# Seven-product matrix steps: another order of the products, and room for weight tiles counted by the tiles in use

## The chip, the cores and the metric

The kernel runs on one core of a Trainium2 chip. The metric is device time in microseconds of one execution, as the median of several runs. Matrix products run on PE (its weight loads are shown as PEld); VectorE (DVE), ScalarE (ACT) and GpSimd (POOL) do the element-wise work; SyncE (SP) issues the transfers (DMA) between device memory and the core's memory SBUF. Matrix products write to PSUM, from which DVE and ACT read.

## What is computed

One layer of a hybrid decoder, for a prompt of 2048 tokens and 8 requests with 4 new tokens each (32 "sample" tokens), with 1024 features, in float32:

```python
h = x + mixer(rmsnorm(x))                # gated linear attention and a spatial gate, w_in, w_out
h = h + mem_attend(rmsnorm(h))           # attention over 256 memory tokens
g = hn @ w_gate                          # hn = rmsnorm(h); w_gate, w_up: 1024 x 2816
c = conv_b + sum(conv_w[j] * gp[:, j:j + T] for j in range(3))   # gp: two older rows, then g
h = h + (gelu(c) * (hn @ w_up)) @ w_down
y = rmsnorm(h)
```

The change lies in the products with `w_gate` and `w_up`.

## The kernel before

**Tiling.** The prompt is worked through in four blocks of 512 tokens (block 0 to 3). Activations stand with features on the 128 partitions and tokens along a row. Every float32 operand is split into a high part, rounded to the format that PE takes at full rate, and a low rest; `mm3` (lines 92 to 95) adds three products: high × high (L93), high × low (L94), low × high (L95). A split takes ACT for the high part (L85) and DVE for the rest (L86). The sample tokens go through the feed-forward part with block 2, whose rows are then 544 tokens long; their memory attention (`sqp`, `kTp`, `ssc`, a softmax `sp`, `sop`) is spread through the feed-forward part of block 1 as side work.

**Seven products.** In blocks 1 to 3 the products with `w_gate` (`gate7`, names `wg<block><step>`) and `w_up` (`upp7`, names `wup<block><step>`) take a form with seven block products in place of eight. A step yields two tiles of 128 output features for all tokens of the block; there are 11 steps of each kind per block. The weights of a step are three plain tiles (A11, A12, A22, stored by block 0 already split, names ending in `A`) and four sums (S1 with S4, S2 with S3: two raw tiles, names `w_…S`, which are split after loading). The tokens stand in two halves of H columns (256, or 272 in block 2) and in sums of them (`w1`, `wb`, `wu`, `wt`). `seven_step` (line 222) makes one `Step` per product, `part` (line 282):

- the products add up in four chains, x: A11, S2, S3; y: S1, S4; z: A12; w: A22. Each product is 12 matmuls (4 slices × 3).
- With H = 256 (`joint`: blocks 1 and 3) x and w share one bank of PSUM, z and y another, so a step holds two of the four banks `acc`; with 272 columns each chain has its own. A bank carries the name of the chain that is opened first in it. The first matmul in a bank clears it (`fresh`, L297).
- After A11, S1, S2 and A22, ACT copies the chain as it then stands into a quarter of the result (L304); after S3 and S4, DVE adds x to both tiles' halves (L310) and y and z to the first tile (L313). Then `use` runs: gate, convolution and GELU, or the product of the two branches.
- The first gate step of each block (`early`) has an order and code of its own, and the first up step runs `then` after S1: it makes the scale of the tokens' norm and lets the first gate's result go on.

**What sets the order.** The code lists steps (`run`, line 516); the framework then orders the instructions of each engine by its own estimate and may put another step's product between two of one step. A matmul that writes a bank and a copy that reads that bank are kept apart, also where they touch different columns. All transfers of weights are issued by SP, in a fixed order (`fetch`, line 107), each when the tile that it fills is free.

**Room for weights.** There are NW = 10 SBUF tiles for weights ready to use and NR = 4 for raw ones. `run` walks over the steps and, ahead of them, makes units of weights. A plain tile takes 1 of the 10, a split one 2 (`ring`). It notes for each unit the count of tiles made up to it, and stops when the tiles made since the oldest unit still in use would pass 10: a unit that is done counts as long as an older one is in use. A sums unit is in use until its second product (`until`). Raw units that are used without a split (`held`) are counted in the same way against the 4.

Of the kernel before, what the change touches and what calls it, by code (L numbers as in the profile page):

```python
# [13 lines left out]
ALU = mybir.AluOpType  # L14
# [16 lines left out]
NU, NT, NW, NR = 49, 8, 10, 4  # L31
# [6 lines left out]
def hymba_step_kernel(  # L38
# [10 lines left out]
    act, dve, pool, pe = nc.scalar, nc.vector, nc.gpsimd, nc.tensor  # L49
# [21 lines left out]
    def acc(name):  # L71
        return accp.tile([128, 512], F32, tag="acc", name=name)
# [24 lines left out]
    def W(name):  # L97
        return wp.tile([128, 1024], F32R, tag="w", name=name)

    def unit_of(make, ring=2, raw=None, held=False):  # L100

        return NS_(make=make, ring=ring, raw=raw, held=held, until=None)

    in_turn = mybir.DependencyInfo(mybir.DependencyClass.NoSync, mybir.DependencyReason.DATA)
    before = []
# [54 lines left out]
    def seven_tile(src, name):  # L160

        def load():
            t = W(name).rearrange("p (x k m) -> p x k m", x=2, k=4)
            fetch(t.bitcast(F32), src)
            return t
        return unit_of(load, 1)
# [47 lines left out]
    def sums_unit(src, k, name):  # L214

        def raw():
            t = raw_tile(name)
            fetch(t, src)
            return t.rearrange("p (k m) -> p k m", k=k)
        return unit_of(lambda raw: wsplit(raw, name), 2, raw)  # L220

    def seven_step(plain, sums, get_xs, H, outs, use, name, early=False, then=None):


        seq = ("A11", "S1", "A12", "S2", "S3", "S4", "A22") if early else ("A11", "A12", "S2", "S1", "A22", "S3", "S4")
        joint = 2 * H <= 512
        tiles = {}

        def unit(nm):
            if nm in PLAIN:  # L230
                return seven_tile(plain[:, PLAIN.index(nm)], f"{name}{nm}")
            i = SUMS.index(nm)
            return sums_unit(sums[:, i:i + 2].rearrange("p s k m -> p (s k m)"), 8, f"{name}{nm}")

        def hold(nm, w):
            if nm in PLAIN:
                tiles[nm] = w[:, 0], w[:, 1]
            else:
                for j in range(2):
                    tiles[SUMS[SUMS.index(nm) + j]] = tuple(w[x][:, 4 * j:4 * j + 4] for x in range(2))  # L240

        def mm(bank, nm, k, fresh, stop):
            wh, wl = tiles[nm]
            mm3(bank, wh[:, k], wl[:, k], *get_xs()[k][nm], fresh, stop, not early)

        def quarters(q):
            return [q[i // 2][:, (i % 2) * H:(i % 2 + 1) * H] for i in range(4)]

        loads = [nm for nm in seq if nm in PLAIN or SUMS.index(nm) % 2 == 0]
        last = 3  # L250

        if early:
            def fn(*ws):
                for nm, w in zip(loads, ws):
                    hold(nm, w)
                q = outs()
                q0, q1, q2, q3 = quarters(q)
                ps = {nm: (mps if i > 3 else acc)(f"a_{name}{nm}")[:, :H] for i, nm in enumerate(seq)}
                for nm in seq:
                    for k in range(last):  # L260
                        mm(ps[nm], nm, k, k == 0, False)
                for nm in seq:
                    mm(ps[nm], nm, last, False, True)
                    if nm == "A11":
                        act.activation(q0, ps[nm], AF.Copy)
                    elif nm == "S2":
                        dve.tensor_tensor(q3, ps[nm], q0, ALU.add)
                        dve.tensor_tensor(q0, ps["A12"], q0, ALU.add)
                    elif nm == "S3":
                        dve.tensor_tensor(q1, ps["S1"], q3, ALU.add)  # L270
                        dve.tensor_tensor(q2, ps[nm], q3, ALU.add)
                        dve.tensor_tensor(q3, ps[nm], q1, ALU.add)
                    elif nm == "S4":
                        dve.tensor_tensor(q1, ps[nm], q1, ALU.add)
                    elif nm == "A22":
                        dve.tensor_tensor(q2, ps[nm], q2, ALU.add)
                use(*q)
            return Step(fn, [unit(nm) for nm in loads])

        st = NS_()  # L280

        def part(nm, *ws):
            i = CHAIN[nm]
            if nm in loads:
                hold(nm, *ws)
            if nm == "A11":
                st.q, st.at = outs(), {}
            if i not in st.at:
                if joint:
                    t = acc(f"a_{name}{i}")  # L290
                    for n, o in enumerate("xw" if i in "xw" else "zy"):
                        st.at[o] = t[:, n * H:(n + 1) * H]
                    if i in "zy":
                        st.zy = t[:, 0:2 * H]
                else:
                    st.at[i] = acc(f"a_{name}{i}")[:, :H]
            fresh = nm in ("A11", "A12") or not joint and nm in ("S1", "A22")  # L297
            for k in range(last + 1):
                mm(st.at[i], nm, k, fresh and k == 0, k == last)
            if then and nm == "S1":  # L300
                then()
            q = st.q
            if nm in COPIED:
                act.activation(quarters(q)[COPIED[nm]], st.at[i], AF.Copy)  # L304
            elif nm == "A12" and not joint:
                q0 = quarters(q)[0]
                dve.tensor_tensor(q0, st.at["z"], q0, ALU.add)
            elif nm == "S3":
                q23 = q[1].rearrange("p (s t) -> p s t", s=2)
                dve.tensor_tensor(q23, st.at["x"].unsqueeze(1).broadcast_to([128, 2, H]), q23, ALU.add)  # L310
            elif nm == "S4":
                if joint:
                    dve.tensor_tensor(q[0], st.zy, q[0], ALU.add)  # L313
                else:
                    q1 = quarters(q)[1]
                    dve.tensor_tensor(q1, st.at["y"], q1, ALU.add)
                use(*q)

        parts = {nm: Step(lambda *ws, nm=nm: part(nm, *ws), [unit(nm)] if nm in loads else []) for nm in seq}
        for nm in SUMS[::2]:  # L320
            parts[nm].units[0].until = parts[SUMS[SUMS.index(nm) + 1]]
        return Step(None, parts=list(parts.values()))
# [65 lines left out]
    for l in range(7):  # L388
# [3 lines left out]
        v = mf[:, :64].rearrange("p (n h) -> p n h", h=half)  # L392
# [100 lines left out]
    class Step:  # L493
        def __init__(self, fn, units=(), parts=None):
            self.fn, self.units = fn, [wunit(*u) if isinstance(u, tuple) else u for u in units]
            self.parts = parts or [self]
# [19 lines left out]
    def run(steps):  # L516


        steps = [p for st in steps for p in st.parts]
        index = {st: i for i, st in enumerate(steps)}  # L520
        queue = [(i, u) for i, st in enumerate(steps) for u in st.units]
        raws = [(i, u) for i, u in queue if u.raw]
        ready, ring, held, loaded = {}, [], [], {}
        made = at = nraw = done = 0

        def fetched(upto):

            nonlocal nraw
            while nraw < min(upto, len(raws)):
                i, u = raws[nraw]  # L530
                if held and nraw - held[0][0] >= NR:
                    break
                if u.held:
                    held.append((nraw, index[u.until] if u.until else i))
                loaded[id(u)] = u.raw()
                nraw += 1

        for i, st in enumerate(steps):
            now[0] = i
            flush(i - 1)  # L540
            for live in (ring, held):
                while live and live[0][1] < i:
                    live.pop(0)
            while at < len(queue):
                j, u = queue[at]
                if ring and made + u.ring - ring[0][0] > NW:
                    break
                if u.raw:
                    fetched(done + 2)
                    if id(u) not in loaded:  # L550
                        break
                    done += 1
                if u.ring:
                    ring.append((made, index[u.until] if u.until and not u.held else j))
                ready.setdefault(j, []).append(u.make(*([loaded.pop(id(u))] if u.raw else [])))
                made += u.ring
                at += 1
            assert len(ready.get(i, ())) == len(st.units)
            st.fn(*ready.pop(i, []))
# [1327 lines left out]
```

## Time and profile before

| what | us |
|---|---|
| median of 3 runs | 2861.88 (2861.6 to 2862.01) |
| the profiled execution | 2856.59 |
| its span, first to last instruction | 2854.9 |
| PE busy in the span | 2803.4 (98%) |
| DVE, ACT, POOL busy | 1844.4, 1215.6, 576.0 |

How to read the rows. In a list of groups or of waits, `PE a_wg36x L93 <- DMA wg36A<-w7g` says that line 93 on PE, writing `a_wg36x`, stood idle until the transfer into `wg36A` had landed; then come the total, the number and the longest in microseconds. `a_wg36x` is the bank opened by chain x of gate step 6 of block 3. In a time line a row has the start in microseconds, the duration, engine, line, operation, output and inputs, shapes and count, and in brackets the idle time before it and what ended it. In a table by stretches a row has the stretch, its length, then busy time and number of instructions of PE, PEld, DVE, ACT and POOL, the granted clock of PE as a share of the full one, the busy share of the DMA engines and their GB/s.

### The profile page before, as it was taken

What the parts mean: (1) busy time and instruction counts of PE and PEld (TensorE: products, weight loads), DVE (VectorE), ACT (ScalarE), POOL (GpSimd) and SP (SyncE); (2) the same over time, 40 slices, a digit from 0 to 9 for tenths busy, and PEclk for the clock granted to TensorE, in tenths of its full rate; (3) what the DMA queues carried; (4) which work ended last, traced back from release to release, by engine and by line L of the source; (5) the groups of instructions that cost most, each with busy time, mean ns of one, the idle gap of its engine ahead of it and who ended that gap; (6) DMA issues with size and microseconds to landing.
All of it is one profiled execution on the core that took longest, in us unless ns stands there. A gap on an engine that the chain in (4) does not pass through costs nothing.

```text
span 2854.9 us, 46641 instructions
## 1 busy us (share of the span) xinstructions
PE 2803.4 (98%) x17894; PEld 2476.6 (87%) x17894; DVE 1844.4 (65%) x3054; ACT 1215.6 (43%) x2185; POOL 576.0 (20%) x638
## 2 busy tenths in 40 slices
PE   8999999999999999999999999999999999999998
PEld 8888888888878898888888879899999888899997
DVE  6588767677646876555455777755556776655565
ACT  5645543323453354333334445533333544533333
POOL 2002112111111321222220121322221122132232
PEclk9999999999999999999999999999999999999999
DMA  9766589999732255776885216566665324566664
GB/s 302 231 191 222 180 272 310 322 313 315 257 98 68 86 187 187 285 251 227 284 303 176 82 45 221 184 227 233 216 236 192 92 69 139 194 236 216 241 242 164
DMA packets 348212, 592.03 MB, mean 207 GB/s; under 512 B 25610, under 2 KB 225388, under 8 KB 347990
## 3 DMA queue, kind: packets, MB, share of 16 engines
q1 hardware_dynamic: 347990, 589.06, 61.3%
q8 instruction: 141, 2.31, 0.3%
q14 instruction: 81, 0.66, 0.1%
HBM read 473.09 MB, written 115.87 MB: 206 GB/s over the span
## 4 chain that ended last, share of the span: by engine, by line
PE 84%; DMA 5%; DVE 5%; ACT 2%; issue 1%; POOL 1%; SPq 0%; POOLq 0%; ACTq 0%; DVEq 0%
PE d L95 6%; PE d L94 6%; PE d L93 6%; PE a_wx L93 2%; PE a_wx L95 2%; PE a_wx L94 2%; PE s L1101 2%; PE a_wg L93 1%; PE a_wg L95 1%; PE a_wup L93 1%; PE a_wup L95 1%; PE a_wg L94 1%; PE a_wup L94 1%; PE a_wo L93 1%; PE a_wu L93 1%
## 5 line engine op out<-in xcount | busy, mean ns | idle before, releaser
L93 PE MATMUL d<-acth,h_wd 128*128 128x512 f32 (+1 forms) x864 | 303.8, 353 | 0.9 <-DMA h_wd<-wd 0.9
L94 PE MATMUL d<-actl,h_wd 128*128 128x512 f32 (+1 forms) x864 | 302.4, 350 | 0.0
L95 PE MATMUL d<-acth,l_wd 128*128 128x512 f32 (+1 forms) x864 | 302.3, 351 | 0.0
L1736 DVE TENSOR_TENSOR h<-d,h 128x512 f32<-128x512 f32 (+1 forms) x232 | 134.8, 584 | 154.9 <-PE d L95 154.2
L93 PEld LDWEIGHTS d<-acth,h_wd 128*128 128x128 f32 x864 | 162.3, 188 | 22.5 <-PE sqp L1446 1.4
L95 PEld LDWEIGHTS d<-acth,l_wd 128*128 128x128 f32 x864 | 162.2, 188 | 22.4 <-issue 0.8
L94 PEld LDWEIGHTS d<-actl,h_wd 128*128 128x128 f32 x864 | 162.5, 188 | 21.3 <-issue 0.8
L1631 POOL TENSOR_TENSOR c<-c,bc_f 128x512 f32<-128x512 f32 (+1 forms) x88 | 128.8, 1469 | 130.3 <-ACT c L1630 130.2
L1621 ACT ACTIVATE c<-g,colsb 128x512 f32<-128x512 f32 x88 | 70.4, 811 | 125.9 <-DVE g L1582 83.3
L1653 POOL TENSOR_TENSOR c<-q,c 128x512 f32<-128x512 f32 (+1 forms) x33 | 46.5, 1411 | 377.6 <-DVE q L310 261.0
L93 PE MATMUL a_wo<-ch,h_wo 128*128 128x512 f32 (+1 forms) x320 | 114.0, 367 | 0.7 <-ACT ch L89 0.4
L94 PE MATMUL a_wo<-cl,h_wo 128*128 128x512 f32 (+1 forms) x320 | 113.4, 357 | 0.0
L95 PE MATMUL a_wo<-ch,l_wo 128*128 128x512 f32 (+1 forms) x320 | 112.4, 355 | 0.0
L85 ACT ACTIVATE acth<-c 128x512 fp32r<-128x512 f32 (+1 forms) x88 | 55.4, 636 | 129.6 <-POOL c L1653 50.8
L1618 POOL COPY carry<-g 128x2 f32<-128x2 f32 x88 | 42.9, 492 | 324.4 <-DVE g L1582 276.0
L95 PE MATMUL a_wx<-pTh,l_wx 128*128 128x512 f32 x256 | 100.2, 394 | 0.0
L94 PE MATMUL a_wx<-pTl,h_wx 128*128 128x512 f32 x256 | 99.9, 393 | 0.0
L93 PE MATMUL a_wx<-pTh,h_wx 128*128 128x512 f32 x256 | 99.0, 394 | 0.0
L86 DVE TENSOR_TENSOR actl<-c,acth 128x512 fp32r<-128x512 f32 (+1 forms) x88 | 63.9, 728 | 39.8 <-ACT acth L85 39.2
L1622 DVE SCALAR_TENSOR_TENSOR c<-g,colsb,c 128x512 f32<-128x512 f32 x88 | 72.1, 827 | 14.7 <-ACT c L1621 14.6
L1630 ACT ACTIVATE c<-c 128x512 f32<-128x512 f32 (+1 forms) x88 | 55.0, 634 | 56.9 <-DVE c L1623 53.8
L1623 DVE SCALAR_TENSOR_TENSOR c<-g,colsb,c 128x512 f32<-128x512 f32 x88 | 76.7, 881 | 1.2
(4117 smaller groups left out, 9542.8 us busy)
## 6 DMA issues: line engine op xcount, KB each, us to landing
h_wd<-wd SPq DMA_DIRECT2D x66, 512.0 KB
l_wd<-wd SPq DMA_DIRECT2D x66, 512.0 KB
w_wo<-in_w_out_dram SPq DMA_DIRECT2D x32, 512.0 KB
h_wx<-vod SPq DMA_DIRECT2D x32, 512.0 KB
l_wx<-vod SPq DMA_DIRECT2D x32, 512.0 KB
w_wg<-in_w_gate_dram SPq DMA_DIRECT2D x22, 512.0 KB
w_wup<-in_w_up_dram SPq DMA_DIRECT2D x22, 512.0 KB
w_wd<-in_w_down_dram SPq DMA_DIRECT2D x22, 512.0 KB
```

The lines of the kernel that those rows point to most:

```text
L85: act.activation(hi, src, AF.Copy)
L86: (lo_eng or dve).tensor_tensor(lo, src, hi.bitcast(F32), ALU.subtract)
L93: pe.matmul(ps, wh, xh, start=first, stop=False, skip_group_check=again)
L94: pe.matmul(ps, wh, xl, start=False, stop=False, skip_group_check=again)
L95: pe.matmul(ps, wl, xh, start=False, stop=last, skip_group_check=again)
L1101: pe.matmul(ps3[:, :, c * 64:(c + 1) * 64], kl[:, c * 128:(c + 1) * 128], kr3[:, :, c * 64:(c + 1) * 64], start=True, stop=True)
L1621: act.activation(c[:, :SB], g[:, 2:SB + 2], AF.Identity, bias=cb, scale=w2)
L1622: dve.scalar_tensor_tensor(c[:, :SB], g[:, 1:SB + 1], w1, c[:, :SB], ALU.mult, ALU.add)
L1623: dve.scalar_tensor_tensor(c[:, :SB], g[:, 0:SB], w0, c[:, :SB], ALU.mult, ALU.add)
L1630: act.activation(c[:, :T], c[:, :T], AF.Gelu_apprx_tanh)
L1631: pool.tensor_tensor(c[:, :T], c[:, :T], B.fbc[:, :T], ALU.mult)
L1736: dve.tensor_tensor(B.h[m + mm][:, cs], ps[:, :cw], B.h[m + mm][:, cs], ALU.add)
```

## The change

Two things change.

**The order of the products** in `seven_step`, outside the early step: from A11, A12, S2, S1, A22, S3, S4 to A11, S1, A12, A22, S2, S4, S3. The first four each begin a chain, the last three add to one. With it go which product clears a bank, and the end of a step: the addition of y (and z) follows S4 and is no longer last, the addition of x to both tiles follows S3, and `use` runs there. The bank that was named z is now opened by y. Weights are loaded in the order of their use, so S1's raw tile is now loaded before S2's.

**The count of room**: `ring` and `held` become tables of the units in use with the step up to which each is; a new unit fits when the tiles of the units in use and its own are at most 10 together. A raw unit that is held counts from when it is taken up, together with the raw tiles loaded and not yet taken. For this a unit becomes an object of a class of its own. Line numbers shift by 3 or 4.

```diff
-        seq = (... "S4", "A22") if early else ("A11", "A12", "S2", "S1", "A22", "S3", "S4")
+        seq = (... "S4", "A22") if early else ("A11", "S1", "A12", "A22", "S2", "S4", "S3")
...
-            fresh = nm in ("A11", "A12") or not joint and nm in ("S1", "A22")
+            fresh = nm in ("A11", "S1") or not joint and nm in ("A12", "A22")
...
+            elif nm == "S4" and joint:
+                dve.tensor_tensor(q[0], st.zy, q[0], ALU.add)
+            elif nm == "S4":
+                q1 = quarters(q)[1]
+                dve.tensor_tensor(q1, st.at["y"], q1, ALU.add)
             elif nm == "S3":
                 q23 = q[1].rearrange("p (s t) -> p s t", s=2)
                 dve.tensor_tensor(q23, st.at["x"].unsqueeze(1).broadcast_to([128, 2, H]), q23, ALU.add)
-            elif nm == "S4":
-                if joint:
-                    dve.tensor_tensor(q[0], st.zy, q[0], ALU.add)
-                else:
-                    q1 = quarters(q)[1]
-                    dve.tensor_tensor(q1, st.at["y"], q1, ALU.add)
                 use(*q)
...
-                if held and nraw - held[0][0] >= NR:
+                if len(held) + nraw - done >= NR:
                     break
...
             for live in (ring, held):
-                while live and live[0][1] < i:
-                    live.pop(0)
+                for u in [u for u in live if live[u] < i]:
+                    del live[u]
...
-                if ring and made + u.ring - ring[0][0] > NW:
+                until = index[u.until] if u.until else j
+                if ring and sum(v.ring for v in ring) + u.ring > NW:
                     break
...
-                if u.ring:
-                    ring.append((made, index[u.until] if u.until and not u.held else j))
+                ring[u] = j if u.held else until
```

The instructions of every engine are the same in kind and number. Up to block 1's feed-forward part their order is the same too, but for a few transfers that trade neighbours; from there on it differs within the feed-forward parts of blocks 1, 2 and 3.

More of the change, by code (lines that the diff above doesn't have):

```diff
@@ L98, in W, with __init__ @@
         return wp.tile([128, 1024], F32R, tag="w", name=name)
+    class Unit:
+        def __init__(self, make, ring, raw, held):
+            self.make, self.ring, self.raw, self.held, self.until = make, ring, raw, held, None
     def unit_of(make, ring=2, raw=None, held=False):
-        return NS_(make=make, ring=ring, raw=raw, held=held, until=None)
+        return Unit(make, ring, raw, held)
     in_turn = mybir.DependencyInfo(mybir.DependencyClass.NoSync, mybir.DependencyReason.DATA)
@@ L222, in seven_step @@
     def seven_step(plain, sums, get_xs, H, outs, use, name, early=False, then=None):
-        seq = ("A11", "S1", "A12", "S2", "S3", "S4", "A22") if early else ("A11", "A12", "S2", "S1", "A22", "S3", "S4")
+        seq = ("A11", "S1", "A12", "S2", "S3", "S4", "A22") if early else ("A11", "S1", "A12", "A22", "S2", "S4", "S3")
         joint = 2 * H <= 512
@@ L522, in run @@
         raws = [(i, u) for i, u in queue if u.raw]
-        ready, ring, held, loaded = {}, [], [], {}
-        made = at = nraw = done = 0
+        ready, loaded = {}, {}
+        ring, held = {}, {}
+        at = nraw = done = 0
         def fetched(upto):
@@ L530, in fetched @@
                 i, u = raws[nraw]
-                if held and nraw - held[0][0] >= NR:
+                if len(held) + nraw - done >= NR:
                     break
-                if u.held:
-                    held.append((nraw, index[u.until] if u.until else i))
-                loaded[id(u)] = u.raw()
+                loaded[u] = u.raw()
                 nraw += 1
@@ L549, in run @@
                     fetched(done + 2)
-                    if id(u) not in loaded:
+                    if u not in loaded:
                         break
                     done += 1
-                if u.ring:
-                    ring.append((made, index[u.until] if u.until and not u.held else j))
-                ready.setdefault(j, []).append(u.make(*([loaded.pop(id(u))] if u.raw else [])))
-                made += u.ring
+                    if u.held:
+                        held[u] = until
+                ring[u] = j if u.held else until
+                ready.setdefault(j, []).append(u.make(*([loaded.pop(u)] if u.raw else [])))
                 at += 1
```

## The prediction

> **What bounds the kernel now.** I read the page first, then the idle time of each engine in the stretches that the change touches, then the chain of waits of PE, then single rows on the time line.
>
> ```profile
> span 2854.9 us, 46641 instructions
> PE 2803.4 (98%) x17894; PEld 2476.6 (87%) x17894; DVE 1844.4 (65%) x3054; ACT 1215.6 (43%) x2185; POOL 576.0 (20%) x638
> PE 84%; DMA 5%; DVE 5%; ACT 2%; issue 1%; POOL 1%; SPq 0%; POOLq 0%; ACTq 0%; DVEq 0%
> ```
>
> PE is busy 2803.4 of 2854.9 us and holds 84% of the chain that ended last. The change adds and removes no matmul, copy, addition or byte, so it can only move PE's idle time. The seven-product form is used in the feed-forward parts of blocks 1, 2 and 3 (`a_wg1…`, `a_wup1…` and so on). Their three stretches, with PE's busy time first:
>
> ```profile
> 1120.00:1500.00 380.00, 368.13 (x2811) 325.84 (x2810) 204.31 (x253) 136.13 (x233) 92.51 (x108) 1.00 0.76 267
> 1825.00:2115.00 290.00, 289.64 (x2314) 289.23 (x2314) 170.91 (x289) 111.11 (x199) 82.25 (x119) 1.00 0.62 222
> 2490.00:2805.00 315.00, 310.20 (x2227) 290.57 (x2227) 181.65 (x224) 118.29 (x197) 89.10 (x89) 1.00 0.67 233
> ```
>
> PE idles 380 - 368.1 = 11.9 us in block 1, 0.4 us in block 2 and 4.8 us in block 3: 17 us in all, which is nearly the ceiling of what the change can give. What ended these waits (total, times, longest):
>
> ```profile
> PE a_wup15x L93 <- ACT q L304: 3.1, 1, 3.1
> PE a_wg36x L93 <- DMA wg36A<-w7g: 1.5, 1, 1.5
> PE a_wg16z L93 <- DVE g L310: 1.2, 1, 1.2
> PE a_wg16z L95 <- DVE l_wg16S L86: 1.2, 1, 1.2
> ...
> PE a_wup32z L93 <- ACT q L304: 0.9, 1, 0.9
> PE a_wup110x L93 <- ACT q L304: 0.8, 1, 0.8
> PE a_wg18z L93 <- DMA wg18A<-w7g: 0.8, 1, 0.8
> PE a_wup19x L93 <- ACT q L304: 0.7, 1, 0.7
> PE a_wg18x L93 <- DMA wg18A<-w7g: 0.7, 1, 0.7
> PE a_wg34x L93 <- DMA wg34A<-w7g: 0.7, 1, 0.7
> PE a_wg14z L93 <- DMA wg14A<-w7g: 0.6, 1, 0.6
> ...
> PE a_wg310x L93 <- DMA wg310A<-w7g: 0.5, 1, 0.5
> PE a_wup13x L93 <- DMA wup13A<-w7u: 0.5, 1, 0.5
> PE a_wg32x L93 <- DMA wg32A<-w7g: 0.5, 1, 0.5
> PE a_wg38x L93 <- DMA wg38A<-w7g: 0.5, 1, 0.5
> PE a_wg12x L93 <- DMA wg12A<-w7g: 0.4, 1, 0.4
> ```
>
> Two kinds matter: weights that land late (DMA), and a copy or addition out of PSUM that comes late (ACT, DVE). The idle column understates each wait:
>
> ```profile
> 2652.68 0.28 PE L94 MATMUL a_wup35z<-wtlwx,h_wup35S 128*128 128x256 f32 x1
> 2652.80 0.28 PE L95 MATMUL a_wup35z<-wthwx,l_wup35S 128*128 128x256 f32 x1
> 2654.62 0.36 PE L93 MATMUL a_wg36x<-w1wx,wg36A 128*128 128x256 f32 x1 [1.55 <-DMA wg36A<-w7g]
> ```
>
> Matmuls start 0.12 us apart but are shown 0.28 us long. The stall is 2654.62 - 2652.80 - 0.12 = 1.70 us where 1.55 is listed, so I add 0.16 to each wait. One product is 12 matmuls, 1.4 us.
>
> **Loads ahead of the gate products, block 3.** The transfers of gate pair 36 left SP's queue thus:
>
> ```profile
> 2648.71 0.80 SPq L109 DMA_DIRECT2D wg36A<-w7g  x2
> 2649.55 0.42 SPq L109 DMA_DIRECT2D w_wg36S<-s7g  x1
> 2650.07 0.38 SPq L109 DMA_DIRECT2D w_wup36S<-s7u  x1
> 2657.93 0.32 SPq L109 DMA_DIRECT2D wg36A<-w7g  x1
> ```
>
> Four transfers of 512 KB (A11, A12, S1, the next S2) start within 1.4 us, and A11 is there only when PE goes on at 2654.6: 5.9 us for a load that shares the DMA engines with three others. SP's queue at this place, before and after (A11, A12, A22 are the plain tiles, S1 and S2 the sums, g the gate, u or up the up-projection):
>
> ```order
> L109 DMA w_wup35S1_27078<-s7u5_198 128x1024
> L109 DMA w_wg36S2_27149<-s7g6_200 128x1024
> L109 DMA wup35A22_27155<-w7u5_197 128x1024
> L109 DMA wg36A11_27186<-w7g6_199 128x1024
> L109 DMA wg36A12_27188<-w7g6_199 128x1024
> L109 DMA w_wg36S1_27206<-s7g6_200 128x1024
> L109 DMA w_wup36S2_27277<-s7u6_202 128x1024
> L109 DMA wg36A22_27283<-w7g6_199 128x1024
> ```
>
> ```order
> L113 DMA wup35A22_27110<-w7u5_197 128x1024
> L113 DMA w_wg36S1_27151<-s7g6_200 128x1024
> L113 DMA wg36A11_27157<-w7g6_199 128x1024
> L113 DMA w_wg36S2_27188<-s7g6_200 128x1024
> L113 DMA wg36A12_27210<-w7g6_199 128x1024
> L113 DMA wg36A22_27238<-w7g6_199 128x1024
> L113 DMA w_wup36S1_27279<-s7u6_202 128x1024
> ```
>
> S1 now goes ahead of A11, and A12 no longer rides beside it. The programs' semaphores tell which matmul frees the tile that a load takes over. For A11 of gates 34, 36, 38 little changes: 37 matmuls lie between that one and A11's own first before, 38 after (36 for gate 310, 49 for 32 both times). So the count by tiles in use does not bring A11 forward; what changes is its company. A12 is freed 28 matmuls (3.3 us) after A11, so A11 and S2 share the engines alone. By bytes, half of four transfers' 5.9 us is 3 us; the bounds are 3.0 and 5.9, and I take 4.0, since part of the 5.9 is not transfer but start and finish. The lead is 38 × 0.12 = 4.6 us. The five waits (1.5, 0.7, 0.5, 0.5, 0.5, plus 5 × 0.16 = 4.5 us) shrink to some 0.5: gain **4.0** (bounds 0 and 4.5).
>
> **Loads, block 1.** By the same counts gates 12 (third plain tile), 14 (A12) and 18 (A12) get 57 or more matmuls of lead and lose 0.4 + 0.6 + 0.8 + 0.5 = **2.3** (bounds 1 and 2.3). `wg18` A11 and `wup13` A11 keep theirs (36 and 42 matmuls). Two leads get short: A11 of gate 16 has 28 matmuls, 3.3 us (48 before), and the last down-projection's low tile in block 3 has 26. Against 4.0 us needed I charge **0.5** each; the far bound is 5.9 - 3.2 = 2.7 each.
>
> **Copies out of PSUM.** For 256 tokens a step has two banks: x|w and z|y. A product that adds to a bank must wait for the copy that reads it. In the new list A12 follows S1 and S2 follows A22 in one bank; before, S3 followed A22. The order fills these places: counted on PE's queue in blocks 1 and 3, waits on a copy or addition less than 2.6 us after the product that it reads go from 27 + 3 to 10 + 5. `wup19` loses its wait (three products and narrow work now lie between A11 and A22, two before between A11 and S2): 0.7 + 0.16 = 0.9. `wup110` keeps one product between, so I leave its 0.8. The wait of `wup32` has another cause:
>
> ```profile
> 2571.87 1.06 ACT L85 ACTIVATE h_wg33S<-w_wg33S 128x1024 fp32r<-128x1024 f32 x1 [5.69 <-DMA w_wg33S<-s7g]
> 2572.83 0.37 ACT L304 ACTIVATE q<-a_wup32z 128x256 f32<-128x256 f32 x1
> ```
>
> ACT stood behind the split of a sums tile that had not landed, and the copy behind that. This can fall on another copy as well; I count half of 1.06. Sum **1.4** (bounds 0 and 3).
>
> **Block 1 around the softmax of the sample tokens.** ACT's queue here, `sp` the softmax, `q` and `g` copies of up 15 and gate 16:
>
> ```order
> L1630 ACTIVATE c_13406<-c_13406 128x512
> L1517 ACT_TABLE_LOAD
> L1517 ACTIVATE sp,smx<-ssc,smx,srp 128x256
> L304 ACTIVATE q_13438<-a_wup15x 128x256
> L304 ACTIVATE q_13439<-a_wup15z 128x256
> L304 ACTIVATE g_13564<-a_wg16x 128x256
> ```
>
> ```order
> L1633 ACTIVATE c_13408<-c_13408 128x512
> L1520 ACT_TABLE_LOAD
> L1520 ACTIVATE sp,smx<-ssc,smx,srp 128x256
> L308 ACTIVATE q_13442<-a_wup15x 128x256
> L308 ACTIVATE q_13443<-a_wup15y 128x256
> L308 ACTIVATE g_13564<-a_wg16x 128x256
> ```
>
> Four copies stand behind the softmax in both, and PE's next work after the scores `ssc` needs the first of them (S2 before, A22 now). So the largest wait, 3.1 us, **stays**, and so does what follows it:
>
> ```profile
> 1318.00:1325.00 7.00, 2.73 (x29) 1.75 (x28) 3.72 (x7) 3.33 (x7) 1.83 (x4) 0.99 0.25 75
> 1325.00:1328.40 3.40, 3.40 (x16) 3.40 (x17) 0.25 (x1) 1.15 (x4) 0.00 (x0) 0.52 0.00 0
> ```
>
> After the wait the granted clock is 0.52 for 3.4 us, and 16 matmuls take 0.21 us each: 16 × 0.09 = 1.5 us more. It is in the time before and after alike. [...]
>
> The two waits of `wg16z` ahead of the scores (1.2 on an addition, 1.2 on a split, 0.3 hidden) lose their cause: A12 now stands after the softmax, and the load of S1 has 10.8 us of PE work between its buffer and its use where it had 6.8. Part may come back as S1's wait for its bank: gain **2.0** (bounds 0 and 2.7).
>
> **Narrow passes.** Sample products of 32 columns break into the wide ones:
>
> ```profile
> 1160.98 0.28 PE L95 MATMUL a_wup11x<-wuhwx,wup11A 128*128 128x256 f32 x1
> 1161.19 0.63 PE L1446 MATMUL sqp<-w_sq,smpx 128*32 128x256 f32 x6
> 1161.75 0.38 PE L93 MATMUL a_wup11z<-wbhwx,h_wup11S 128*128 128x256 f32 x1
> ```
>
> The order has 5 passes of `sqp` for 7 and 17 of `sop` for 19, with as many matmuls. A break costs between 0.09 (0.21 for 0.12 on entry) and 0.77 us (the whole pass); I take 0.33, so 4 × 0.33 = **1.3**.
>
> **What is added.** The last product is now S3, and its addition frees the bank that S1 of the next gate needs:
>
> ```profile
> 2649.94 0.28 PE L95 MATMUL a_wg35x<-wthwx,l_wg35S 128*128 128x256 f32 x1
> 2651.75 0.68 DVE L310 TENSOR_TENSOR g<-a_wg35x,g 128x512 f32<-128x512 f32 x1
> ```
>
> At gates 34, 36, 38 and 310 some 20 to 22 matmuls (2.4 to 2.6 us) lie between, 38 before (where A12 needed it). Before, S3 of gate 35 ended at 2649.94 + 0.28 = 2650.2 and its addition at 2651.75 + 0.68 = 2652.4, behind other work of DVE: 2.2 us, so the cover just holds. 0 to 1 us each; I charge 4 × 0.3 = **1.2**. For copies that fall late elsewhere I charge **0.8**. In block 2 (four banks, 272 columns) the waits sum to 0.4 us, and I count nothing either way. At the start of each block the late gate's scale is asked for 36 matmuls (4.3 us) after the sums of squares instead of 48; its chain on DVE and POOL runs beside them, and if that cover failed it would show once a block.
>
> Sum: 4.0 + 2.3 + 1.4 + 2.0 + 1.3 = 11.0 gone, 0.5 + 0.5 + 1.2 + 0.8 = 3.0 new: **-8.0 us**. The profiled execution took 2856.59 us (span 2854.9 and 1.7 around it), so 2848.6; the median, 2861.88, lies 5.3 above it, so **2853.9**. A measurement of this kernel tells about 0.2%, 5.7 us, from no change.
>
> **The rivals.**
> 1. *The loads are not earlier.* 37 against 38 matmuls: if a lone pair of transfers also needs over 5 us, the five waits of block 3 stay and half of block 1's. Then -8.0 + 4.0 + 1.2 = -2.8: 2859.1. For it: the unchanged lead. Against it: four transfers then, two now.
> 2. *The waits only change places.* The order deals ACT's and DVE's queues anew, and as much falls late as is gained: 2861.9. For it: `wup32`, where the delay came from elsewhere.
> 3. *Slower: the shared bank.* A12 waits for the copy of S1, S2 for that of A22, with two products (2.9 us) between. It decides when ACT starts such a copy over 2.9 - 0.4 = 2.5 us late, as behind the split above (5.69 us idle). One wait like that of `wup32` (0.9) in each of 16 of the 20 pairs of steps in blocks 1 and 3: +14.4 - 8.0 = +6.4: 2868.3. Against it: the counted distances grow. [...]
>
> **How the numbers follow.** Forecast 0.60, rival 1 0.17, rival 2 0.15, rival 3 0.08. Faster by over 0.2%: 0.9 of the forecast and 0.15 of rival 1, 0.57. Slower: rival 3, 0.08. The rest is 0.35. The low end: everything gone that can go (4.5 + 2.3 + 3 + 2.7 + 1.9 = 14.4) with nothing new: 2847.5. The high end takes in rivals 1 and 2 with a microsecond: 2863.0; rival 3 and a few from the forecast's far bounds are left out.
>
> **What would show it.** Right: the five DMA waits of block 3's gates below 0.3 us each; no wait of `wg16` on DVE; `wup15` still waits about 3 us with the clock near 0.5 behind it; PE's idle time 3 to 4 us shorter in block 1 and 3 to 4 in block 3. Wrong: the gates' waits as long as before (rival 1), PE waiting for L308 or L319 in many steps (rival 3), or any change in block 2 or outside the feed-forward parts.

## The result, and the profile after

The changed kernel is slower: 2873.93 us as the median of 5 runs, against 2861.88 us for 5 runs of before between them. The ratio is 1.0039, with a 95% interval of 1.0024 to 1.0053. The forecast was 2853.9, with a range up to 2863.0.

The profiled execution after, with PE's longest waits below it (total, times, longest):

```profile
span 2871.9 us, 46605 instructions
PE 2808.6 (98%) x17894; PEld 2480.4 (86%) x17894; DVE 1834.3 (64%) x3054; ACT 1216.4 (42%) x2185; POOL 568.2 (20%) x638
```

```profile
PE a_wup15x L93 <- ACT q L308: 3.1, 1, 3.1
...
PE sqf L1458 <- DVE sqt L1453: 2.7, 1, 2.7
...
PE a_wg16x L93 <- DVE c L1625: 2.4, 1, 2.4
PE a_wg11x L93 <- DMA wg11A<-w7g: 2.4, 1, 2.4
...
PE a_wup21x L93 <- ACT q L308: 1.6, 1, 1.6
...
PE a_wg110x L93 <- DVE c L1626: 1.4, 1, 1.4
PE a_wg38x L93 <- DMA wg38A<-w7g: 1.4, 1, 1.4
PE a_wup30y L93 <- ACT q L308: 1.2, 1, 1.2
PE a_wg18x L93 <- DMA wg18A<-w7g: 1.1, 1, 1.1
PE a_wup21w L93 <- DVE g L319: 1.0, 1, 1.0
PE ncp L1798 <- POOL carry L1621: 0.9, 2, 0.5
PE d L95 <- DMA l_wd<-wd: 0.8, 1, 0.8
PE a_wup13x L93 <- ACT q L308: 0.8, 1, 0.8
PE a_wg31x L93 <- DMA wg31A<-w7g: 0.7, 1, 0.7
PE a_wg36x L93 <- DMA wg36A<-w7g: 0.6, 1, 0.6
```

`wup15` waits 3.1 us as before. The waits at the starts of the blocks (`wg11`, `wup21`, `wup30`, `wg31`) are new, and so is that of `sqf` in the side work. The loads of gates 36 and 38 are still waited for. The row of `wg16x` names an operation of DVE that has no part in that product. Its A11 had left at 1320.37, the last part of it landed at 1325.90, 0.14 us before PE went on, and the addition that frees the bank had ended at 1325.34: this wait, too, is one for a load.

**Where the 17 us between the two profiles are.** I take, for each matmul, the time from its start to the next one's start, less the median of that time for its shape (0.119 us for 256 columns). Summed over a part of the program this is its *excess*: what PE lost there to waits, breaks and a lower clock. In the feed-forward parts it went from 45.3 to 53.0 us in block 1, from 1.7 to 4.4 in block 2 and from 6.5 to 10.4 in block 3: +14.3. (The profile of before is of an execution 5.3 us below its median, hence 17 between the profiles and 12 between the medians.) The part ahead of block 1's feed-forward went from 58.0 to 62.2, with the same order of instructions but for a few transfers. In the profiles of the experiments that part has 58.6 to 68.4, slow kernels and fast, so I put those 4.2 us down to scatter of a single execution. The parts behind the feed-forward parts make up the rest, some -1.5 us.

**The start of block 1.** First SP's queue before, then after. The loads of the first up step are A11 and A12, then S2 before; after they are A11, S1, then A12.

```profile
1113.25 5.44 SPq L109 DMA_DIRECT2D wup10A<-w7u  x2
1118.74 0.42 SPq L109 DMA_DIRECT2D w_wup10S<-s7u  x1
1119.27 0.38 SPq L109 DMA_DIRECT2D w_sq<-in_wq_x_dram  x1
1127.83 0.32 SPq L109 DMA_DIRECT2D wup10A<-w7u  x1
```

```profile
1117.26 0.38 SPq L113 DMA_DIRECT2D wup10A<-w7u  x1
1117.69 0.42 SPq L113 DMA_DIRECT2D w_wup10S<-s7u  x1
1130.42 0.79 SPq L113 DMA_DIRECT2D wup10A<-w7u  x2
1131.32 0.93 SPq L113 DMA_DIRECT2D w_sq<-in_wq_x_dram  x2
1132.35 0.54 SPq L113 DMA_DIRECT2D w_wg11S<-s7g  x1
1132.98 0.42 SPq L113 DMA_DIRECT2D wg11A<-w7g  x1
```

The longest wait of SP's queue there, after:

```profile
SPq L113 <- PE a_wg10A L95: 12.6, 1, 12.6
```

Before, both plain tiles had left by 1118.7, and the queue stood from 1119.65 to 1127.83. After, A12 finds no tile free: the queue stands 12.6 us, and everything behind it (the sample's `w_sq`, the sums and A11 of gate 11) leaves in a bunch from 1130.4 on. Stretches of the changed kernel, with PE's granted clock, DMA share and GB/s at the end of each row:

```profile
1140.00:1144.00 4.00, 1.74 (x8) 1.75 (x9) 3.75 (x5) 2.96 (x5) 3.96 (x4) 0.71 1.02 412
1144.00:1148.00 4.00, 4.00 (x31) 4.00 (x31) 1.36 (x3) 2.64 (x4) 0.74 (x2) 0.86 0.85 283
...
1164.00:1168.00 4.00, 1.85 (x9) 1.79 (x10) 2.77 (x4) 1.95 (x5) 3.56 (x3) 0.70 0.65 252
1168.00:1172.00 4.00, 4.00 (x27) 2.73 (x27) 2.10 (x3) 1.40 (x2) 2.57 (x4) 0.50 0.00 0
```

The DMA engines are full (share 1.02), A11 of gate 11 lands 2.4 us late (9.2 us after it left), and the clock is lower behind that wait (0.57 from 1142.2 to 1145.6), as it is again behind that of `sqf` (0.50 from 1168 to 1172).

**The loads of block 3.** SP's queue after, at gate 36, the DMA share there, and PE's first matmul with A11:

```profile
2659.33 0.80 SPq L113 DMA_DIRECT2D wup35A<-w7u  x2
2660.22 0.38 SPq L113 DMA_DIRECT2D w_wg36S<-s7g  x1
2663.71 0.32 SPq L113 DMA_DIRECT2D wg36A<-w7g  x1
2664.12 0.49 SPq L113 DMA_DIRECT2D w_wg36S<-s7g  x1
```

```profile
2661.00:2663.00 2.00, 2.00 (x19) 2.00 (x18) 0.37 (x1) 1.84 (x3) 0.93 (x1) 1.00 0.97 373
2663.00:2665.00 2.00, 2.00 (x19) 2.00 (x18) 1.73 (x3) 0.00 (x0) 0.00 (x0) 1.00 0.94 375
```

```profile
2668.72 0.36 PE L93 MATMUL a_wg36x<-w1wx,wg36A 128*128 128x256 f32 x1 [0.59 <-DMA wg36A<-w7g]
```

A11 does not share the engines with S2 alone: S1 and two plain tiles of the up step left 3.5 to 4.4 us ahead of it, and the last parts of one plain tile and of S1 land 0.7 and 2.0 us after A11 has left. It is there when PE goes on at 2668.72, 5.0 us after its issue; before it was 5.9.

### The profile page after: what moved, and what is told of

It reads as the page before. It is cut to its first block, busy times and chain, and to the rows that moved or that the text cites. A ratio compares the mean times of both kernels' runs of the same rounds, so it can differ in the third digit from the quotient of the medians.

```text
span 2871.9 us, 46605 instructions
## 1 busy us (share of the span) xinstructions
PE 2808.6 (98%) x17894; PEld 2480.4 (86%) x17894; DVE 1834.3 (64%) x3054; ACT 1216.4 (42%) x2185; POOL 568.2 (20%) x638
## 4 chain that ended last, share of the span: by engine, by line
PE 86%; DVE 5%; DMA 4%; ACT 2%; issue 1%; POOL 1%; SPq 0%; POOLq 0%; ACTq 0%; DVEq 0%
PE d L93 6%; PE d L95 6%; PE d L94 6%; PE a_wx L93 2%; PE a_wx L94 2%; PE a_wx L95 2%; PE s L1104 2%; PE a_wg L93 1%; PE a_wup L93 1%; PE a_wg L95 1%; PE a_wup L95 1%; PE a_wg L94 1%; PE a_wup L94 1%; PE a_wo L93 1%; PE a_wu L93 1%
## 5 line engine op out<-in xcount | busy, mean ns | idle before, releaser
L93 PE MATMUL d<-acth,h_wd 128*128 128x512 f32 (+1 forms) x864 | 304.3, 354 | 0.0
L94 PE MATMUL d<-actl,h_wd 128*128 128x512 f32 (+1 forms) x864 | 302.8, 351 | 0.0
L93 PEld LDWEIGHTS d<-acth,h_wd 128*128 128x128 f32 x864 | 162.4, 188 | 22.5 <-issue 1.4
L94 PEld LDWEIGHTS d<-actl,h_wd 128*128 128x128 f32 x864 | 162.5, 188 | 20.5 <-issue 0.4
L93 PE MATMUL a_wo<-ch,h_wo 128*128 128x512 f32 (+1 forms) x320 | 114.2, 369 | 0.5 <-ACT ch L89 0.3
L94 PE MATMUL a_wo<-cl,h_wo 128*128 128x512 f32 (+1 forms) x320 | 113.0, 356 | 0.2 <-POOL cl L86 0.2
L94 PE MATMUL a_wx<-pTl,h_wx 128*128 128x512 f32 x256 | 99.9, 393 | 0.0
L93 PE MATMUL a_wx<-pTh,h_wx 128*128 128x512 f32 x256 | 99.1, 395 | 0.0
```

The lines of the kernel that those rows point to most:

```text
L93: pe.matmul(ps, wh, xh, start=first, stop=False, skip_group_check=again)
L94: pe.matmul(ps, wh, xl, start=False, stop=False, skip_group_check=again)
```

## The experiments

Times are medians of 4 to 12 runs, the difference is to the median of before in the same series, the ratio has its 95% interval, and the last columns are the excess of one profile in the feed-forward parts of blocks 1, 2 and 3.

| run | order, loads, count | us | to before | ratio | excess 1 / 2 / 3 |
|---|---|---|---|---|---|
| before | | | | | 45.3 / 1.7 / 6.5 |
| the change | A11 S1 A12 A22 S2 S4 S3 | 2873.93 | +12.1 | 1.0039 (1.0024-1.0053) | 53.0 / 4.4 / 10.4 |
| e1 | new order, old count | 2873.96 | +14.8 | 1.0049 (1.0035-1.0063) | 56.7 / 4.6 / 11.6 |
| e2 | old order, new count | 2857.49 | -1.7 | 0.9993 (0.9984-1.0002) | 41.3 / 1.6 / 6.8 |
| e3 | first steps old | 2870.16 | +11.0 | 1.0031 (1.0017-1.0044) | 52.4 / 3.1 / 11.1 |
| e4 | new in block 3 alone | 2859.62 | +0.5 | 1.0000 (0.9991-1.0009) | 42.0 / 1.7 / 9.5 |
| e5 | half tiles, new order | 2878.20 | +18.9 | 1.0065 (1.0050-1.0081) | 59.2 / 2.0 / 16.2 |
| e6 | half tiles, old order | 2860.46 | +1.2 | 1.0002 (0.9993-1.0010) | 46.2 / 3.7 / 6.8 |
| e7 | side work ahead, new order | 2932.79 | +73.5 | 1.0257 (1.0241-1.0273) | 11.5 / 4.8 / 9.8 |
| e8 | side work ahead, old order | 2923.71 | +64.4 | 1.0220 (1.0203-1.0238) | 9.7 / 1.9 / 6.2 |
| e9 | A11 A12 S2 S1 A22 S4 S3 | 2860.50 | +0.5 | 1.0005 (0.9995-1.0016) | 42.2 / 4.8 / 8.0 |
| e10 | A11 S1 A12 A22 S2 S3 S4 | 2872.29 | +12.3 | 1.0051 (1.0038-1.0063) | 50.0 / 5.6 / 8.9 |
| e11 | A11 A12 S1 A22 S2 S4 S3 | 2853.26 | -6.8 | 0.9977 (0.9967-0.9988) | 40.7 / 2.8 / 1.2 |
| e12 | A11 A12 A22 S1 S2 S4 S3 | 2845.52 | -14.5 | 0.9956 (0.9941-0.9972) | 37.1 / 4.9 / -0.5 |
| e13 | new order, A12 loaded ahead of S1 | 2875.57 | +16.7 | 1.0062 (1.0046-1.0078) | 51.4 / 5.9 / 10.0 |
| e14 | e11, S1 loaded ahead of A12 | 2869.93 | +11.1 | 1.0039 (1.0027-1.0052) | 46.8 / 4.1 / 11.3 |
| e15 | e12, old count | 2847.93 | -10.9 | 0.9964 (0.9951-0.9976) | 39.9 / 6.1 / -0.6 |
| e16 | e12, nine tiles | 2858.47 | -0.4 | 1.0004 (0.9995-1.0012) | 41.3 / 9.3 / 6.2 |
| e17 | e12, S1 loaded ahead of A22 | 2842.37 | -19.7 | 0.9932 (0.9920-0.9944) | 36.0 / 5.6 / -1.2 |
| e18 | e12, block 2 as before | 2845.33 | -16.7 | 0.9943 (0.9930-0.9955) | 36.2 / 0.9 / -0.6 |

**e1 and e2: order or count.** The first has the `run` of before with the new `seven_step`, the second the `run` of after with the old products.

```diff
-        seq = (...) if early else ("A11", "S1", "A12", "A22", "S2", "S4", "S3")
+        seq = (...) if early else ("A11", "A12", "S2", "S1", "A22", "S3", "S4")
```

> The new order of the products with the old count of room. All theories set against the kernel before on the same chip (2861.9 us at the forecast). Theory (the starts): the loss is made by the new order in the first up step and the first ordinary gate step of a block, where the loads bunch up; the count does nothing. Then this kernel is as slow as the full change: +10 to +14 us, with the waits of a_wg11x on its load (2.4) and of the sample step sqf (2.7) near 1140 and 1166 us and half clock behind them. Rival (the count): the new count of room lets transfers leave at worse moments. Then this kernel is within 4 us of before and these waits are gone. Rival (chance): part of the +17 us of the one profile is scatter of one execution, the +4 us before the changed part above all; then that +4 does not come back here.

> The old order of the products with the new count of room. Theory (the starts, made by the order): within 3 us of the kernel before, block 1 to 3 with the same waits as before (a_wup15x 3.1, a_wg36x 1.5). Rival (the count): +8 to +14 us, with the two new waits near 1140 and 1166 us. If the few early transfers that trade neighbours under the new count cost the +4 us that the changed kernel has lost by 330 us, this kernel shows +4 us there too.

The order alone is as slow as the change, the count alone is at -1.7 us, with an interval that includes no change at all. So the loss is the order's.

**e3 and e4: where.** The old order by the name of the step:

```diff
+        old = name in ("wup10", "wg11", "wup20", "wg21", "wup30", "wg31")      # e3
+        old = not name.lstrip("wgup").startswith("3")                          # e4
```

> The full change, but the first up step and the first ordinary gate step of each of the three blocks keep the old order (6 of 63 steps). Theory (the starts): the waits of a_wg11x (2.4), sqf (2.7), a_wup21w and a_wup21x (2.6) and a_wup30y and a_wg31x (1.9) go, with half clock of some 2 us: 9 to 12 us faster than the full change, so between -1 and +4 us against before. Rival (late copies everywhere): the loss is spread over the steps; then at most 3 us are won, +9 us or more against before.

> The new order in block 3 alone, with the new count; blocks 1 and 2 keep the old order. In the profile of the full change block 3 lost some 4 to 5 us: the waits on its gates' loads fell only from 3.7 to 2.3 (listed), and waits on copies and on the carry transposes came in. Theory: +3 to +6 us against before, all of it after 2490 us, half of it in its first two steps and half in the odd steps, where narrow carry transposes and copies stand ahead of the next gate. Rival (loads were won, and only the start lost): -2 to +2 us.

My theory of the starts fell: e3 is the change with the old order in its first steps, and it is at +11.0 where the change is at +12.1, with intervals that overlap. Block 1's excess stays at 52.4, where the change has 53.0. The wait of `wg11` is gone in its profile, but `sqf` still waits 2.2, and `wup15` (4.1) and `wg18` (2.8) wait longer. So no part of the loss is shown to be that of the starts. In e4 the theory of +3 to +6 us was missed as well: against before nothing shows (+0.5). Against e2, which has the same count, the loss of block 3 is 2.7 us in the profile and 2.1 us by the medians of the two (2859.62 - 2857.49), with intervals that overlap. So most of the loss lies in blocks 1 and 2, above all in block 1.

**e5 to e8: bytes, or the side work.**

```diff
-            t = W(name).rearrange("p (x k m) -> p x k m", x=2, k=4)            # e5, e6
-            fetch(t.bitcast(F32), src)
+            t = W(name).rearrange("p (x k m) -> p x k m", x=2, k=4)[:, :, 0:2]
+            fetch(t.bitcast(F32), src[:, :, 0:2])
...
-            sides.append((sample_steps(), 1, len(fmain) - 5))                  # e7, e8
+            steps += sample_steps()
```

> Leaves out half of the bytes of every plain tile in blocks 1 to 3 (A11, A12, A22: 256 KB in place of 512 KB; the products read the loaded half twice, with as many matmuls), in the new order with the new count. Read against the same with the old order, in the same series. So far the new order costs 11 to 14 us, nearly all of it in blocks 1 and 2, and in block 1 the waits on A11 of gates 11, 12, 16, 18 and 110 add up to 6 to 12 us where the old order has some 4. Theory (loads): these loads come late because the room is full and the queue of SP stands; with half the bytes the waits fall below 3 us, and new minus old is below 6 us. Rival (copies): DVE and ACT are late by the order in which the copies, splits and additions stand; then new minus old stays at 9 us or more.

> The same halved plain tiles with the old order of the products and the new count: the counterpart of the kernel with the new order. Both theories: some 3 to 6 us faster than before, since the waits on plain tiles (4 in block 1, 4 in block 3) mostly go.

> The whole of the sample tokens' memory attention (the side work of block 1) is done ahead of block 1's feed-forward part and not spread through it; new order, new count. Read against the same with the old order. Theory (side work): the new order loses in block 1 because the side work's loads stand in the same queue of SP and its narrow passes and copies between the products; without it block 1 is like block 3, where the order alone cost nothing that shows (0.5 us): new minus old is below 4 us. Rival (the order itself, or the room at the start): new minus old stays at 9 us or more, with the wait of a_wg11x on its load.

> The sample tokens' memory attention ahead of block 1's feed-forward part, with the old order of the products and the new count: the counterpart. Both theories: slower than before by 20 us or more, because the side work's waits stand alone on the path; only the difference between this kernel and the one with the new order counts.

Halving the bytes does not shrink the difference between the orders (17.7 us, where it is 13.8 between the change and e2): the loss does not go by bytes. By the lines drawn ahead this spoke for late copies and against late loads; e14 below speaks for the loads again. e6 missed too: the old order with half tiles was to be 3 to 6 us faster than before and is not (+1.2). (A half tile takes a whole place in the room, so the moments at which loads leave stay; that this is why was not tried by itself.) With the side work out of block 1 the difference is 9.1 us by the medians: the line that I had drawn at 4 was missed, and the rival's line of 9 is met, though without the wait of `wg11` that was its sign. But in block 1 the excess differs by 1.8 us only, where it is 11.7 with the side work (53.0 against 41.3 of e2; 7.7 against the 45.3 of before). The rest is blocks 2 and 3, which keep their +2.9 and +3.6. So in block 1, by these single profiles, the new order loses where it meets the side work. The side work's loads go through the same queue of SP; that this is why was not tried by itself.

**e9 to e12: start or end of the step.** Only `seq` is changed, with the first product in each bank clearing it and `use` after the last:

```diff
+        seq = ... ("A11", "A12", "S2", "S1", "A22", "S4", "S3")    # e9
+        seq = ... ("A11", "S1", "A12", "A22", "S2", "S3", "S4")    # e10
+        seq = ... ("A11", "A12", "S1", "A22", "S2", "S4", "S3")    # e11
+        seq = ... ("A11", "A12", "A22", "S1", "S2", "S4", "S3")    # e12
```

> The old order but for its last two products: A11, A12, S2, S1, A22, S4, S3, with the new count. So far: the old order with the new count is at -1.6 us against before, the new order at +12 to +14, and by the profiles block 1 loses 11 us, block 2 3 and block 3 3 to 4. Theory (the end): a step that ends on S3, whose addition holds back the result and the x bank, makes the loss; then this kernel is +6 us or more. Rival (the start: S1 second, so that its two tiles and its load go ahead of A12): this kernel is within 3 us of before.

> The new order with the old end: A11, S1, A12, A22, S2, S3, S4, with the new count. Theory (the end): within 5 us of before. Rival (the start): +9 us or more, as the full change.

> A12 put back ahead of S1 in the new order: A11, A12, S1, A22, S2, S4, S3, with the new count. S1's two tiles are then taken one product later and the loads of A11 and A12 stand together as before. Rival (the start): within 5 us of before. Theory (the end), or the four openings with two copies into shared banks: +8 us or more.

> All three plain products first: A11, A12, A22, S1, S2, S4, S3, with the new count. Each sum tile pair is then in use for three products (five and three in the full change, four and four before), so that the room of ten fills less: product-tiles in use 15 a step where both other orders have 19. If room for weights is what makes the loads late, this is the best of all, -3 us or better against before. If copies into shared banks or the end on S3 make the loss, it is +5 us or more.

This is clean: the end on S3 does nothing that shows, in either setting. With A12 put back in second place the kernel is faster than before (by 6.8 us, where my line was 5 us either way), and with all plain products first it is faster by 14.5 us. The loss comes from S1 as the second product.

**e13 to e16: loads and room, or the order on PE.** A step takes up the units of two products, in the order given; the later product uses what was kept:

```diff
+        taken = {"S1": ("A12", "S1"), "A12": ()}       # e13, products as in the change
+        taken = {"A12": ("S1", "A12"), "S1": ()}       # e14, products as in e11
-NU, NT, NW, NR = 49, 8, 10, 4                          # e16, products as in e12
+NU, NT, NW, NR = 49, 8, 9, 4
```

> The products in the order of the full change (A11, S1, A12, A22, S2, S4, S3), but A12's tile is taken and loaded ahead of S1's. Theory (loads and room): S1's two tiles and its load ahead of A12 are the cause; then this kernel loses at most 3 us against before and may gain. Rival (products on PE: copies, shared banks): as the full change, +10 us or more.

> The products in the order A11, A12, S1, A22, S2, S4, S3 (at -6.8 us against before), but S1's tiles are taken and loaded ahead of A12's. Theory (loads and room): slow, +5 us or more against before. Rival (products on PE): still -4 us or better.

> The order with the plain products first (A11, A12, A22, S1, S2, S4, S3; -14.5 us with the new count) with the old count of room. The old count stops at the oldest unit in use; in this order S1's tiles are behind the plain ones, so few units are done while an older one is in use. If the count has no part: within 3 us of -14.5. If tiles done early matter: -10 us or worse.

> The order with the plain products first with nine weight tiles in place of ten, new count. Theory (loads and room): loads become late again; at least 8 of the 14.5 us are lost, with DMA waits of the gates' A11. Rival (products on PE): at most 4 us are lost.

e14 has e11's list of products, and only the loads of S1 and A12 change places: -6.8 becomes +11.1. (The framework then puts some 560 of PE's 17894 matmuls at other places.) PE's longest waits in block 3, first the longest of e11, then four of e14 (from 2490 us on):

```profile
PE a_wg310z L93 <- DVE g L319: 0.4, 1, 0.4
```

```profile
PE a_wg38z L93 <- DMA wg38A<-w7g: 2.4, 1, 2.4
PE a_wg36z L93 <- DMA wg36A<-w7g: 2.2, 1, 2.2
PE a_wg310z L93 <- DMA wg310A<-w7g: 2.2, 1, 2.2
PE a_wg34z L93 <- DMA wg34A<-w7g: 2.1, 1, 2.1
```

`z` is the bank of A12. SP's queue at gate 36, again e11 and e14:

```profile
2638.68 1.62 SPq L113 DMA_DIRECT2D wg36A<-w7g  x2
2640.39 0.38 SPq L113 DMA_DIRECT2D w_wg36S<-s7g  x1
```

```profile
2655.73 0.32 SPq L113 DMA_DIRECT2D wg36A<-w7g  x1
2656.14 0.38 SPq L113 DMA_DIRECT2D w_wg36S<-s7g  x1
2662.72 0.80 SPq L113 DMA_DIRECT2D wg36A<-w7g  x2
```

In e11 both plain tiles leave together. In e14 A12 leaves 7.0 us behind A11 (2662.72 against 2655.73), as S1's split has the next two tiles, and the product that follows A11 waits 2.2 us for it. So S1's tiles ahead of A12's are enough to make a loss of this size.

e13 missed: with the products of the change, A12's load ahead of S1's mends nothing. There A11, A12 and both tiles of S1 have to find room by the second product. SP's queue at the start of block 1 stands 7.7 us in e13, as in e11, and `wg11` waits 1.1 where it is 2.4 in the change; yet block 1 keeps its excess (51.4). So the long stand of the queue there is not needed for a loss of this size. Other waits have come: `wg12` 2.6 us for its load in block 1, and in block 3 the carry transposes `ncp` for POOL, 5.9 us in five. Whether this again is room, or whether the products' order on PE costs something by itself, is not told apart: a kernel that uses S1 second and takes its tiles later can't be made. e16 shows that the room is tight in general: the tenth tile is worth 14 us, and waits for the gates' loads come back (`wg110` 1.4, `wg12` 0.8). e15 lies between the lines drawn for it (-10.9); its interval overlaps that of e12, so the count has no part that shows there either.

**e17 and e18: degrees, and a better version.**

```diff
+        taken = {"A22": ("S1", "A22"), "S1": ()}                                # e17, products as in e12
+        seq = ... (plain first) if 2 * H <= 512 else (the order of before)      # e18
```

> The products with the plain ones first (A11, A12, A22, S1, S2, S4, S3; -14.5 us against before), but S1's tiles are taken and loaded ahead of A22's, one product earlier. Theory (loads and room, in degrees): between the best order and the one with A12 second, so -4 to -11 us against before. Rival (the moment does not matter here, since only taking tiles ahead of A12 hurts): within 3 us of -14.5.

> The plain products first in blocks 1 and 3, the order of before in block 2, with the new count. In the profiles block 2 had 1.7 us above the plain sum of its matmuls in the old order and 4.9 with the plain products first. If that difference carries over: -16 to -19 us against before. If not: -14.5 as with the order in all three blocks.

The theory in degrees fell: S1's load one product earlier, but behind A12, costs nothing, and the median is the best of all, better than the rival's line too. The kernels that are slow for their order (the change, e1, e3, e5, e10, e13, e14) have this in common: S1's two tiles must find room by the second product, in all steps or most. Where A12 alone is taken there, none is slow. How long the tiles are held does not order the kernels. Each tile counted by the products of its step for which it is needed, it is 19 a step in before, in the change and in e14, 17 in e11 and e17, and 15 in e12; but e14 loses 11 us against before, and e17 is not slower than e12. e17 beats before by 19.7 us (0.9932) and the change by more than 30. e18 gives block 2 its old excess back (0.9), and -16.7 lies in what was expected, but its interval overlaps those of e12 and e17, so whether block 2 adds to the gain stays open.

## Why the prediction was wrong

The forecast was -8.0 us, the result +12.1. PE was to idle 3 to 4 us less in block 1 and as much less in block 3; its excess there grew by 7.7 and 3.9 us. Of the marks named for wrong, a change in block 2 came, and in part gates that wait for their loads: the listed waits of block 3's five gates fell from 3.7 to 2.2, and were to be below 0.3 each. By its own steps:

- **Loads ahead of block 3's gates, -4.0: failed.** The step said that A11 and S2 then share the engines alone. They don't: S1, moved ahead of A11, and one plain tile of the up step are still under way (share 0.94 to 0.97). The forecast itself noted that S1 now goes first, and did not count its bytes. For A11, 4.0 us were taken and 5.0 measured; `wg36` and `wg38` still wait 0.6 and 1.4. Rival 1 was right here in half: over half of the waits stayed, but not for a lone pair of transfers.
- **Loads of block 1, -2.3, and the charge of 0.5 for gate 16: the charge failed.** The waits of gates 12 and 14 and of A12 of gate 18 went as forecast; that of A11 of gate 18 rose from 0.7 to 1.1. But gate 16, with its lead cut to 28 matmuls, waits 2.4, near the far bound of 2.7: its A11 landed 5.5 us after it left, where 4.0 were taken. The last down-projection's low tile, charged the same 0.5, waits 0.8. Gate 110 waits 1.4, where nothing was listed before.
- **Around the softmax, -2.0: right in its cause, empty in its sum.** Both waits of `wg16z` went, `wup15` still waits 3.1. But the time comes back as gate 16's late A11. I costed the two at different places and did not see that they are one stretch.
- **Copies, -1.4, and the late copies, 0.8: wrong in sign.** Before, the waits on copies listed were 0.9, 0.8 and 0.7. After, they are 1.6 (`wup21x`), 1.2 (`wup30y`), 0.8 (`wup13x`) and more below: without `wup15`, all listed waits on copies went from 3.0 to 5.1. Counting how many copies follow closely on their product said nothing of when ACT gets to them. `wup30y` is a wait of the kind of rival 3, but the sum of them all is far from its 14.4.
- **Narrow passes, -1.3: hidden by more.** The passes of `sqp` and `sop` are fewer, but `sqf` now waits 2.7 for DVE, which stands behind a split of S2's tile, and the carry transposes `ncp` wait 0.9.
- **The addition of S3, 1.2: not seen.** None of the gates 34, 36, 38 and 310 has a listed wait on that addition (L319); the cover held.
- **The start of each block, 0: failed.** It was named as a place to show once a block, for the chain of the scale, and given no price. What shows is the queue of loads: `wg11` 2.4, and copies and additions at `wup21` (2.6), `wup30` (1.2). But e3, with the old order in these steps, does not get the time back.
- **Block 2, 0: failed**, +2.7 us. That the waits were 0.4 before was no reason: `wup21` now waits 1.6 for a copy and 1.0 for an addition. My reading, that four chains which begin one after another want four banks, is not shown: e9, which keeps the old beginning, has 4.8 in block 2 as well.
- **Half clock, not charged.** I had measured 1.5 us of it behind the wait of 3.1 us and charged nothing for new waits. New waits of 2.4 to 2.7 had it behind them too (clock 0.50 to 0.57, below): some 4.7 us in this profile, by my estimate from the spacing of the matmuls behind them.

What failed at the root is the way of counting: I compared the distance of each load from the matmul that frees its tile, load by load, and missed that one unit without room stops the whole queue. That the loads and their room are enough for such a loss is shown by e14; that they are the whole of it in the change itself is not (e13). The order printed showed S1 ahead of A11 and A12; what it meant for A12 and for all that stands behind it was not followed up. Rival 3 had the right sign, with another cause.

## What to carry to other kernels

Where all loads go through one queue in a fixed order, a new order of use is first a new order of claims on the room: ask for each unit how many tiles it takes, what stands behind it in the queue, and how soon that is needed. Units that take two tiles and a split go behind the single tiles that the next products need; here the loads of A12 and S1 changing places was worth 17.9 us, with the same list of products (e14 against e11). Where S1 was used second, the same exchange gained nothing (e13). Price such a change at the starts of the stretches as well, where the room is still full of what came before.

## What the runs showed of the hardware

Before, the wait of 3.1 us had the clock at 0.52 behind it; in the changed kernel shorter waits had it low as well. Two stretches of the changed kernel, behind the waits of `wg11x` and `wg16x`, with the granted clock as the third number from the end:

```profile
1142.20:1145.60 3.40, 3.34 (x17) 3.35 (x18) 3.16 (x5) 1.20 (x4) 2.54 (x4) 0.57 1.04 393
```

```profile
1326.00:1329.00 3.00, 2.96 (x14) 2.99 (x15) 2.60 (x4) 1.33 (x2) 2.77 (x4) 0.51 0.30 120
```

In the changed kernel 13 matmuls behind the wait of `wg11x` (2.4 us) start 0.213 us apart where 0.119 is usual, 1.2 us more. Behind the waits of `wg16x` (2.4) and `sqf` (2.7) it is some 1.3 and 2.2 us. Behind the waits of `wup21x` (1.6), `wg110x` and `wg38x` (1.4) there are none, and the clock stays at 1.00. So the shortest wait of this profile's feed-forward parts with a low clock behind it was 2.4 us, and in one of the two cases narrow sample products stand ahead of it; whether they have a part in it was not tried. Nor does the length of the wait alone decide. A stretch of e3 behind a wait of 1.8 us (`wg310x`), and two of e14 behind waits of 2.2 and 2.4 (`wg36z`, `wg38z`):

```profile
2799.20:2802.60 3.40, 3.38 (x17) 3.40 (x18) 3.25 (x4) 2.26 (x5) 2.21 (x5) 0.55 0.21 86
```

```profile
2666.60:2670.00 3.40, 3.40 (x29) 3.40 (x30) 1.94 (x3) 0.56 (x2) 0.25 (x1) 1.00 0.52 207
2731.50:2735.00 3.50, 3.50 (x30) 3.50 (x31) 1.92 (x3) 0.51 (x2) 0.14 (x1) 1.00 0.43 174
```

The clock is 0.55 behind the shortest of the three and 1.00 behind the other two. So the waits of 2.4 to 2.7 us in the changed kernel cost another 1.2 to 2.2 us each, and two of 2.2 and 2.4 us in e14 nothing by the clock; what decides was not found.

Three readings stand behind what was said of formats, banks and loads. In the profile of before two products of 512 columns in plain float32 take 0.98 us up to the next start (L790, from 813.39 on), two of the rounded parts just ahead of them 0.46 (L93 and L94, from 812.61 on): by "full rate" the second is meant. In the changed kernel A22 of up 15 writes other columns of its bank than A11; PE stands idle 3.1 us ahead of it and starts it at 1334.74, 0.06 us after the end of ACT's copy of A11's columns (1334.31 + 0.37). And a load of 512 KB that left alone, A22 of gate 36 in before at 2657.93, has 0.1 MB moved from 2658.0 to 2659.5 and 0.44 MB in the 1.5 us after that (66 and 295 GB/s): in the first half of its three microseconds little moved.

One part of the program that the change leaves alone had an excess of 58.0 to 68.4 us in the profiles here (without e7 and e8, which put more work there). A difference of 4 us between two single profiles says nothing before it is placed in the program.
